# Token sums of the seven-product feed-forward layers issued earlier, from the rows, and a new order of the seven products

## The chip, the cores and the metric

The kernel runs on one core of one Trainium2 chip. The metric is device time in microseconds (us), from a run without a profile; the median of three runs is compared. TensorE (PE) does the matmuls, VectorE (DVE) and ScalarE (ACT) and GpSimd (POOL) work elementwise, and SyncE (SP) issues the loads.

## What is computed

Two blocks of two layers each on 512 tokens of width 1024. Each of the four layers has a mixer and a feed-forward part; the change touches three of the four feed-forward parts. The reference, cut to them:

```python
def rmsnorm(x, g):
    xf = x.astype(jnp.float32)
    y = xf * lax.rsqrt(jnp.mean(xf * xf, axis=-1, keepdims=True) + EPS)
    return (y * g).astype(x.dtype)

def swiglu_ffn(u, w_gate, w_up, w_down):        # w_gate, w_up: 1024 x 2816, w_down: 2816 x 1024
    return (jax.nn.silu(u @ w_gate) * (u @ w_up)) @ w_down

# first block, layer l:   x = x + g2 * _swiglu(_rms_norm(x, norm_ffn[l]) * (1 + sc2) + sh2, ...)
# second block, layer i:  h = h + swiglu_ffn(rmsnorm(h, ffn_norm[i]), ...)
```

## The kernel before

Activations are kept transposed: channels on the 128 partitions, 512 tokens along the row. The residual stands in `xT`, eight tiles `X[0]` to `X[7]` of 128 channels. Every operand of a matmul is split into two reduced-precision parts, `hi` (a cast on ACT) and `lo` (the difference, on DVE), and a product is three matmuls (`mm3`, L304 to L306): hi by hi, lo of the moving operand by hi, hi by lo of the weights. Weights are loaded by SP into three `raw` buffers and split by `split` (L296 ACT, L297 DVE).

A feed-forward part (`ffn(n, ...)`, n = 0 to 3) has 22 columns j of 128 hidden units. For each it makes a gate tile and an up tile (psum `pg`, `pu`), evacuates them to silu(gate) times up (`s`), and splits that into `d`. After every 5 or 6 columns (`PARTS_S`) come the eight down products (`dn`, psum `pj`) over these columns. Six PSUM banks serve `pg`, `pu` and `pj` in turn.

There are two ways to make a column. The **dense** way (`gu`) takes 48 matmuls of 512 tokens: 2 outputs, 8 channel tiles, 3 passes. The **seven-product** way (`gu7`, `seven`) works on quarters: gate and up weights by their first and second four channel tiles (g1, g2, u1, u2), and the tokens by their first and second 256. Seven products of quarter size, combined by additions, replace eight: 84 matmuls of 256 tokens. For this the weights need four sums (s1 to s4, DVE, per column) and the tokens need four sums `q[0]` to `q[3]` per pair of channel tiles (k, k+4), once per layer for four pairs: `crossed` (L679 to L698). They become `xh` and `xl` (hi and lo parts, 128x1024 each); `cross(i)` names the quarter sum i of all four pairs. `FIRST_S` says how many columns of a layer are dense: all 22 for n = 0, three for n = 1, one for n = 2 and for n = 3.

For n = 1 the norm is a `Split`: the normed rows are built in two halves of 256 tokens (`build`, L471 to L493: `z` on DVE, bias and hi on ACT, lo on DVE for even channel tiles and on POOL for odd ones), and the first two dense columns run half by half (`nm.lin`). For n = 2 and 3 the norm is a `Norm`: the rows are only scaled by the gain, and the reciprocal norm R multiplies the outputs. `finish` (L408) makes R: column sums on PE (`ss`), a chain of 13 small DVE instructions (`rsqrt`), four transposes on PE (`rb`) and a copy on ACT (`R`). It is called in the evacuation of the first column, so that nothing of that column leaves PSUM before R stands.

In `crossed` POOL adds hi and lo back to the row value `z` (L687, eight of 128x512, with three `z` buffers), DVE makes the four sums (L690 to L693, 128x256 each), ACT casts `xh` (L695) and DVE subtracts to `xl` (L696). It is called in the first `gu7`, so after the dense columns and their evacuation in program order. In `seven` the first product is g1 with a quarter of the plain rows; the second is with `cross(0)`, the third and fifth with `cross(1)` and `cross(2)`, the seventh with `cross(3)`, the fourth and sixth with plain rows. Products 1, 3, 5 and 7 share the quarter bank `r1`; after 1, 3 and 5 ACT copies it away (L733, L737, L740) before it is written again.

The program is written in the order of these items. A scheduler then orders each engine's queue from its own estimates; the queues run in order, and each instruction waits for its semaphores.

Of the kernel before, what the change touches and what calls it, by code (L numbers as in the profile page):

```python
# [10 lines left out]
F32 = mybir.dt.float32  # L11
# [3 lines left out]
OP = mybir.AluOpType  # L15
# [5 lines left out]
FIRST_S = (22, 3, 1, 1)  # L21
# [69 lines left out]
def _layout(i):  # L91
# [130 lines left out]
def _program(nc, tc, a, out, stages=STAGES):  # L222
# [207 lines left out]
    class Split:  # L430
        def __init__(self, eps, acol, shcol=None, ahead=None):
            self.eps, self.acol, self.shcol, self.ahead, self.W = eps, acol, shcol, ahead, None
            self.rstd = None
            self.h = []

# [36 lines left out]
        def build(self, hf):  # L472
            o = HALVES[hf]
            for c in range(KC):
# [3 lines left out]
                z = tmp("z")  # L478
# [200 lines left out]
    def crossed(h):  # L679


        out = []
        hv = T // 2
        for k in range(4):
            z1, z2 = tmp("z"), tmp("z")
            for z, c in ((z1, k), (z2, k + 4)):
                G.tensor_tensor(z, h[c][0].bitcast(F32), h[c][1].bitcast(F32), op=OP.add)  # L687
            t = wide1("ws")
            q = [t[:, i * hv:(i + 1) * hv] for i in range(4)]
            V.tensor_tensor(q[0], z1[:, :hv], z1[:, hv:], op=OP.subtract)  # L690
            V.scalar_tensor_tensor(q[1], z2[:, hv:], -1.0, q[0], op0=OP.mult, op1=OP.subtract)
            V.tensor_tensor(q[2], z2[:, hv:], z1[:, hv:], op=OP.subtract)
            V.scalar_tensor_tensor(q[3], q[1], -1.0, z2[:, :hv], op0=OP.mult, op1=OP.subtract)  # L693
            hi, lo = wide1("xh", F32R), wide1("xl", F32R)
            S.copy(hi, t)  # L695
            V.tensor_tensor(lo, t, hi.bitcast(F32), op=OP.subtract)  # L696
            out.append([(hi[:, i * hv:(i + 1) * hv], lo[:, i * hv:(i + 1) * hv]) for i in range(4)])
        return out  # L698
# [5 lines left out]
    def seven(g, u, h, x4):  # L704
# [5 lines left out]
        g1, s1, s2, s4, s3, g2, u1, u2 = [w[:, o:o + 512] for w in (wa, wb, wc, wd) for o in (0, 512)]  # L710
        for t, src in ((g1, g[:, :4]), (wd, u), (g2, g[:, 4:])):
            last_load[0] = nc.sync.dma_start(t, flat(src))
        V.tensor_tensor(s1, u1, u2, op=OP.add)
        ah, al = split(wa, 1024)
        V.tensor_tensor(s2, s1, g1, op=OP.add)
        V.tensor_tensor(s4, s2, g2, op=OP.add)  # L716
        bh, bl = split(wb, 1024)
# [16 lines left out]
        product(r3, ah, al, 4, cross(0), True)  # L734
        S.copy(bu[:, :hv], r3)
        product(r1, bh, bl, 0, cross(1), False)
        S.copy(ua[:, hv:], r1)  # L737
        product(r3, bh, bl, 4, quarter(4, two_), False)
        product(r1, ch, cl, 0, cross(2), False)
        S.copy(bu[:, hv:], r1)  # L740
        product(r2, ch, cl, 4, quarter(4, one_), False)
# [6 lines left out]
    def ffn(n, nm, gcol, nxt):  # L748
        sparse = FIRST_S[n] < FC
        phase("ffn" if sparse else "ffn0")  # L750
        x4 = []
        direct = isinstance(nm, Split)
        h = nm.h
        d = {}

        def gu(js):
            def it():
# [5 lines left out]
                if js[0] == 0 and direct:  # L763
                    nm.lin([gr[:2], gr[2:]])
                else:
                    lin(gr, h)
                if nm.R is None:
                    nm.finish().to_sbuf()
# [17 lines left out]
        def gu7(j):  # L786
            def it():
                if not x4:
                    x4.extend(crossed(h))
# [977 lines left out]
    if stages[0] != "mix0":  # L1767
        phase("ffn")
        consts()
        nc.sync.dma_start(row, a["row"].to_broadcast([128, NROW]))  # L1770
        if stages[0] in STAGES[:4]:
            cond()
            mods()
            _run(chain(md0.stream(range(24)), md1.stream(range(24))))
        nm = norms[stages[0]]().all()
# [43 lines left out]
```

## Time and profile before

| what | us |
|---|---|
| median of three runs | 2718.51 (2717.61 to 2718.73) |
| the profiled execution's own time | 2719.51 |
| its span, first to last instruction | 2717.7 |
| PE busy in the span | 2525.8 (93%) |
| DVE busy | 1987.6 (73%) |
| ACT busy | 1250.1 (46%) |
| POOL busy | 534.6 (20%) |

The three layers with seven products run at 945 to 1317 (n = 1), 1733 to 2102 (n = 2) and 2335 to 2703 (n = 3) us of the span. A window's row gives, for a stretch, the busy time of each engine with the number of instructions, and then PEclk: the granted TensorE clock as a share of 2.4 GHz, so 0.50 is the lower of its two levels (1.2 GHz) throughout. Idle time of an engine stands in square brackets before an instruction, with what ended it.

### The profile page before, as it was taken

The page shows a single profiled execution, that of the slowest core. Times are in us where ns is not written, and L with a number is a line of the kernel's source. Part 1 is how long each engine was busy: PE and PEld are TensorE (multiplying, and loading weights), DVE is VectorE, ACT ScalarE, POOL GpSimd, SP SyncE. Part 2 cuts the span into 40 slices and gives each one's busy share as a digit, 9 for nine tenths or more (in the row PEclk, how much of TensorE's full clock was granted, in tenths as well). Part 3 has the DMA queues.
Part 4 walks back from the last instruction along what each step waited for, and adds up shares of the span by engine and source line. Part 5 has one row for each costly group of instructions (what it writes and reads, how often), then busy time and mean ns, then how long its engine had stood idle before and what let it go on. Part 6 is the DMA issues. An engine that isn't in the chain of part 4 may idle for free.

```text
span 2717.7 us, 39747 instructions
## 1 busy us (share of the span) xinstructions
PE 2525.8 (93%) x15176; PEld 2229.9 (82%) x15176; DVE 1987.6 (73%) x3494; ACT 1250.1 (46%) x2283; POOL 534.6 (20%) x371
## 2 busy tenths in 40 slices
PE   5788989999999879999999999799999987799998
PEld 3666888888888879999788888599998877599997
DVE  7898765555457566667678786788777897778776
ACT  4456643222357534445455444345444544445443
POOL 3345120000113220000100000311013783301102
PEclk9988999999999989999999999899999998899999
DMA  7611025555420113323322121133233210133332
GB/s 263 229 54 39 32 95 200 177 174 190 133 88 24 47 55 106 104 93 103 95 78 72 61 72 61 50 103 107 97 102 109 69 56 16 60 111 99 100 98 85
DMA packets 93519, 265.78 MB, mean 98 GB/s; under 512 B 10256, under 2 KB 12688, under 8 KB 93328
## 3 DMA queue, kind: packets, MB, share of 16 engines
q1 hardware_dynamic: 93328, 263.24, 29.2%
q8 instruction: 119, 1.95, 0.3%
q14 instruction: 72, 0.59, 0.1%
HBM read 261.10 MB, written 2.10 MB: 97 GB/s over the span
## 4 chain that ended last, share of the span: by engine, by line
PE 75%; DVE 13%; issue 3%; POOL 3%; DMA 3%; ACT 3%; POOLq 0%; SPq 0%; DVEq 0%; ACTq 0%
PE pj L304 10%; PE pj L306 10%; PE pj L305 10%; PE pg L304 6%; PE pg L306 6%; PE pg L305 6%; PE pu L306 5%; PE pu L304 5%; PE pu L305 5%; POOL yp L1586 2%; DVE lo L297 2%; DMA araw<-ada 1%; PE pj L1398 1%; PE pj L1399 1%; PE pj L1400 1%
## 5 line engine op out<-in xcount | busy, mean ns | idle before, releaser
L296 ACT CAST hi<-raw 128x1024 fp32r<-128x1024 f32 (+5 forms) x445 | 392.9, 891 | 721.2 <-PE pj L305 262.4
L297 DVE TENSOR_TENSOR lo<-raw,hi 128x1024 fp32r<-128x1024 f32 (+5 forms) x435 | 462.2, 1068 | 146.8 <-ACT hi L296 144.3
L304 PE MATMUL pj<-d,hi 128*128 128x512 f32 (+1 forms) x940 | 353.2, 382 | 3.8 <-DVE xT L677 2.0
L305 PE MATMUL pj<-d,hi 128*128 128x512 f32 (+1 forms) x940 | 355.3, 378 | 0.0
L306 PE MATMUL pj<-d,lo 128*128 128x512 f32 (+1 forms) x940 | 352.8, 380 | 0.0
L745 POOL TENSOR_TENSOR bu<-bu 128x256 f32<-128x256 f32 x61 | 102.0, 1672 | 807.5 <-ACT bu L740 594.3
L304 PE MATMUL pu<-hi 128*128 128x256 f32 (+1 forms) x736 | 229.9, 312 | 3.3 <-DVE z L479 3.2
L306 PE MATMUL pu<-hi,lo 128*128 128x256 f32 (+1 forms) x736 | 229.5, 312 | 0.0
L305 PE MATMUL pu<-lo,hi 128*128 128x256 f32 (+1 forms) x736 | 229.4, 312 | 0.0
L305 PE MATMUL pj<-lo,hi 128*128 128x512 f32 (+2 forms) x520 | 208.0, 400 | 4.4 <-DVE lo L490 2.4
L304 PE MATMUL pj<-hi 128*128 128x512 f32 (+2 forms) x520 | 207.9, 403 | 3.9 <-ACT qk L887 1.2
L304 PE MATMUL pg<-xh,hi 128*128 128x256 f32 x732 | 206.8, 283 | 2.2 <-ACT hi L296 2.2
L304 PEld LDWEIGHTS pj<-d,hi 128*128 128x128 f32 x940 | 176.7, 189 | 38.5 <-DVE xT L677 2.6
L306 PE MATMUL pg<-xh,lo 128*128 128x256 f32 x732 | 206.5, 282 | 0.1
L305 PE MATMUL pg<-xl,hi 128*128 128x256 f32 x732 | 205.8, 281 | 0.0
L306 PE MATMUL pj<-hi,lo 128*128 128x512 f32 (+2 forms) x520 | 205.5, 396 | 0.3 <-DVE lo L297 0.3
L305 PEld LDWEIGHTS pj<-d,hi 128*128 128x128 f32 x940 | 177.3, 189 | 33.8 <-issue 1.0
L306 PEld LDWEIGHTS pj<-d,lo 128*128 128x128 f32 x940 | 177.3, 189 | 33.1 <-issue 0.5
L304 PE MATMUL pg<-hi 128*128 128x256 f32 (+1 forms) x564 | 188.3, 334 | 5.5 <-DVE z L479 4.4
L306 PE MATMUL pg<-hi,lo 128*128 128x256 f32 (+1 forms) x564 | 187.3, 332 | 2.2 <-DVE lo L297 2.2
L305 PE MATMUL pg<-lo,hi 128*128 128x256 f32 (+1 forms) x564 | 187.0, 332 | 0.6 <-DVE lo L490 0.6
L296 ACT CAST hi<-ws 128x1024 fp32r<-128x1024 f32 x122 | 126.9, 1048 | 112.7 <-DVE ws L716 34.8
(471 smaller groups left out, 6406.8 us busy)
## 6 DMA issues: line engine op xcount, KB each, us to landing
raw<-w_gu SPq DMA_DIRECT2D x115, 512.0 KB, 3.6
araw<-ada SPq DMA_DIRECT2D x96, 512.0 KB, 5.9
raw<-w_dn SPq DMA_DIRECT2D x48, 384.0 KB, 3.1
raw<-w_gu SPq DMA_DIRECT2D x61, 256.0 KB, 3.0
ws<-w_gu SPq DMA_DIRECT2D x61, 256.0 KB, 2.9
raw<-w_dn SPq DMA_DIRECT2D x48, 320.0 KB, 2.9
raw<-w_p SPq DMA_DIRECT2D x24, 512.0 KB, 3.5
raw<-w_out SPq DMA_DIRECT2D x32, 256.0 KB, 2.8
```

The source lines that it names most:

```text
L296: S.copy(hi, raw)
L297: (eng or V).tensor_tensor(lo, raw, hi.bitcast(F32), op=OP.subtract)
L304: E.matmul(ps, lh, rh, start=start, stop=False, **k)
L305: E.matmul(ps, lh, rl, start=False, stop=False, **k)
L306: E.matmul(ps, ll, rh, start=False, stop=stop, **k)
L745: G.tensor_tensor(bu[:, :hv], bu[:, :hv], bu[:, hv:], op=OP.add)
L1398: E.matmul(o, xh[:, ts], wh[:, k], start=st_, stop=False, skip_group_check=True)
L1399: E.matmul(o, xh[:, ts], wl[:, k], start=False, stop=False, skip_group_check=True)
L1400: E.matmul(o, xl[:, ts], wh[:, k], start=False, stop=sp, skip_group_check=True)
L1586: G.tensor_tensor(yp[:, sft:], yp[:, sft:], pr[:, sft:], op=OP.add)
```

## The change

- `FIRST_S` is (22, 3, 2, 2): layers 2 and 3 get a second dense column, in place of one of seven products.
- `crossed` handles one pair k at a time and is called from `gu`, right behind the matmuls of a dense column and ahead of its evacuation: for n = 1 all four pairs behind the first two columns, for n = 2 and 3 two pairs behind each of the two dense columns.
- The row values no longer come from hi + lo. For n = 2 and 3 ACT makes them from `X[c]` and the gain (eight of 128x512). For n = 1 `build` leaves its `z` tiles standing in eight buffers (`keep`); the first 256 tokens are filled by POOL from hi + lo, and the bias, where `build` had not added it, is added by ACT.
- `q[0]` and `q[2]` move from DVE to POOL; `xl` moves to POOL for k = 1 and 3.
- In `seven`, g1 and g2 share one raw buffer, loaded by one DMA of 512 KB in place of two of 256 KB, and are split together. The two products of plain rows with g1 and g2 come first. The order behind them is: `cross(0)` and `cross(1)` with s1 and s2, the plain quarter and `cross(2)` with s4 and s3, `cross(3)` with u2.
- The pools: a phase of its own for n = 1 with eight `z` buffers, six in place of three for n = 2 and 3.

The diff, cut to its core:

```diff
-FIRST_S = (22, 3, 1, 1)
+FIRST_S = (22, 3, 2, 2)
...
-                z = tmp("z")
+                z = self.keep[c] if self.keep else tmp("z")
...
+    def crossed(k, z1, z2, pool_lo):
         hv = T // 2
+        t = wide1("ws")
+        q = [t[:, i * hv:(i + 1) * hv] for i in range(4)]
+        G.tensor_tensor(q[0], z1[:, :hv], z1[:, hv:], op=OP.subtract)
+        G.tensor_tensor(q[2], z2[:, hv:], z1[:, hv:], op=OP.subtract)
+        V.scalar_tensor_tensor(q[1], z2[:, hv:], -1.0, q[0], op0=OP.mult, op1=OP.subtract)
+        V.scalar_tensor_tensor(q[3], q[1], -1.0, z2[:, :hv], op0=OP.mult, op1=OP.subtract)
+        hi, lo = wide1("xh", F32R), wide1("xl", F32R)
+        S.copy(hi, t)
+        (G if pool_lo else V).tensor_tensor(lo, t, hi.bitcast(F32), op=OP.subtract)
...
         product(r1, ah, al, 0, quarter(0, one_), True)
         S.copy(ua[:, :hv], r1)
-        product(r3, ah, al, 4, cross(0), True)
+        product(r2, ah, al, 4, quarter(4, one_), True)
+        product(r3, bh, bl, 0, cross(0), False)
         S.copy(bu[:, :hv], r3)
-        product(r1, bh, bl, 0, cross(1), False)
+        product(r1, bh, bl, 4, cross(1), False)
         S.copy(ua[:, hv:], r1)
-        product(r3, bh, bl, 4, quarter(4, two_), False)
-        product(r1, ch, cl, 0, cross(2), False)
+        product(r3, ch, cl, 0, quarter(4, two_), False)
+        product(r1, ch, cl, 4, cross(2), False)
         S.copy(bu[:, hv:], r1)
-        product(r2, ch, cl, 4, quarter(4, one_), False)
         product(r1, uh, ul, 0, cross(3), False)
...
+        def sums(ks):
+            for k in ks:
+                z = []
+                for c in (k, k + 4):
+                    if direct:
+                        z.append(nm.keep[c])
+                        if c % 2 == 0 and nm.shcol:
+                            S.activation(z[-1][:, T // 2:], z[-1][:, T // 2:], AF.Identity, bias=nm.shcol(c))
+                    else:
+                        z.append(tmp("z"))
+                        S.activation(z[-1], X[c], AF.Copy, scale=nm.gcol(c))
+                x4.append(crossed(k, *z, k % 2))
...
+                if sparse and len(x4) < 4:
+                    sums(range(4) if direct else range(2 * js[0], 2 * js[0] + 2))
                 if nm.R is None:
                     nm.finish().to_sbuf()
```

What this moves in the queues, at three places.

DVE in layer 1, just behind the last `lo` of the second half of the rows (lo_8624 in both). Before: the split of the third dense column's weights, the first evacuations, and the token sums (L690, ws) only behind the evacuation of that third column (s_8989).

```order
L297 TENSOR_TENSOR lo_8930<-raw_8927,hi_8929 128x1024
L775 TENSOR_TENSOR s_8913<-s_8913,pu_8645 128x512
L297 TENSOR_TENSOR lo_8936<-raw_8933,hi_8935 128x1024
L389 TENSOR_TENSOR d_8917<-s_8913,d_8916 128x512
L713 TENSOR_TENSOR raw_9048<-raw_9049 128x512
L775 TENSOR_TENSOR s_8920<-s_8920,pu_8659 128x512
L297 TENSOR_TENSOR lo_9057<-raw_9048,hi_9056 128x1024
L389 TENSOR_TENSOR d_8924<-s_8920,d_8923 128x512
L775 TENSOR_TENSOR s_8989<-s_8989,pu_8940 128x512
L690 TENSOR_TENSOR ws_9000<-z_8996 128x256
```

Of the change (there the third column's weights are lo_8978 and lo_8984, and its evacuation comes much later):

```order
L689 SCALAR_TENSOR_TENSOR ws_8923<-z_8664,ws_8923 128x256
L690 SCALAR_TENSOR_TENSOR ws_8923<-ws_8923,z_8664 128x256
L689 SCALAR_TENSOR_TENSOR ws_8932<-z_8665,ws_8932 128x256
L690 SCALAR_TENSOR_TENSOR ws_8932<-ws_8932,z_8665 128x256
L689 SCALAR_TENSOR_TENSOR ws_8943<-z_8666,ws_8943 128x256
L690 SCALAR_TENSOR_TENSOR ws_8943<-ws_8943,z_8666 128x256
L693 TENSOR_TENSOR xl_8929<-ws_8923,xh_8928 128x1024
L693 TENSOR_TENSOR xl_8949<-ws_8943,xh_8948 128x1024
L298 TENSOR_TENSOR lo_8978<-raw_8975,hi_8977 128x1024
L791 TENSOR_TENSOR s_8961<-s_8961,pu_8645 128x512
L689 SCALAR_TENSOR_TENSOR ws_8952<-z_8667,ws_8952 128x256
L298 TENSOR_TENSOR lo_8984<-raw_8981,hi_8983 128x1024
```

The sums now stand ahead of the third column's weights and of every evacuation.

ACT at the start of layer 3 (layer 2 is alike), behind the last cast of the rows (hi_22092 before, hi_21990 of the change). Before: R, the first evacuation, then the four casts of the sums.

```order
L733 COPY ua_22292<-pg_22290 128x256
L426 COPY R_22199<-rb_22194 128x512
L779 ACTIVATE s_22201<-s_22201 128x512
L388 CAST d_22207<-s_22201 128x512
L695 CAST xh_22220<-ws_22215 128x1024
L695 CAST xh_22233<-ws_22228 128x1024
```

Of the change (hi_22239 is the split of the first seven-product column's g1 and g2; L761 makes the row values):

```order
L297 CAST hi_22239<-raw_22233 128x1024
L761 ACTIVATE z_22064<-xT_70,vec_71 128x512
L761 ACTIVATE z_22066<-xT_70,vec_71 128x512
L761 ACTIVATE z_22077<-xT_70,vec_71 128x512
L761 ACTIVATE z_22079<-xT_70,vec_71 128x512
L692 CAST xh_22073<-ws_22068 128x1024
L692 CAST xh_22086<-ws_22081 128x1024
L427 COPY R_22123<-rb_22118 128x512
L761 ACTIVATE z_22197<-xT_70,vec_71 128x512
L761 ACTIVATE z_22199<-xT_70,vec_71 128x512
L761 ACTIVATE z_22210<-xT_70,vec_71 128x512
L761 ACTIVATE z_22212<-xT_70,vec_71 128x512
```

Two pairs go ahead of R, the row values of the other two stand behind it.

PE in layer 3, in the first seven-product column (pg_22259, pu_22260), between its products with `cross(2)` and `cross(3)`, of the change. Here the last matmul of `cross(2)` (weights hi_22251, lo_22252) and the two behind it:

```order
L305 MATMUL pg_22259<-xh_22219,hi_22251 128x256
L306 MATMUL pg_22259<-xl_22220,hi_22251 128x256
L307 MATMUL pg_22259<-xh_22219,lo_22252 128x256
L307 MATMUL pg_22389<-hi_21763,lo_22370 128x256
L305 MATMUL pg_22389<-hi_21770,hi_22369 128x256
```

and 22 matmuls of the next column (pg_22389, pu_22390) later the first of `cross(3)` (weights hi_22255, lo_22256):

```order
L307 MATMUL pu_22390<-hi_21990,lo_22370 128x256
L305 MATMUL pu_22390<-xh_22073,hi_22375 128x256
L306 MATMUL pu_22390<-xl_22074,hi_22375 128x256
L305 MATMUL pg_22259<-xh_22073,hi_22255 128x256
L306 MATMUL pg_22259<-xl_22074,hi_22255 128x256
```

In the program these two products stand next to each other; in the queue a part of the next column stands between them.

## Rows read from the trace of the kernel before

**Rows 1.** The page: busy time, and the granted clock in 40 slices.

```profile
PE 2525.8 (93%) x15176; PEld 2229.9 (82%) x15176; DVE 1987.6 (73%) x3494; ACT 1250.1 (46%) x2283; POOL 534.6 (20%) x371
PEclk9988999999999989999999999899999998899999
```

**Rows 2.** Windows: whole first parts, then steady sevens, then a dense column.

```profile
core 0: us, PE busy (x) PEld busy (x) DVE busy (x) ACT busy (x) POOL busy (x), PEclk, DMA share, GB/s
959.30:1035.30 76.00, 62.02 (x423) 57.49 (x422) 54.49 (x75) 34.76 (x55) 17.35 (x14) 0.87 0.20 63
1733.40:1819.90 86.50, 68.42 (x476) 63.72 (x477) 71.53 (x107) 39.44 (x61) 20.41 (x13) 0.86 0.22 69
2334.60:2420.90 86.30, 68.70 (x479) 63.91 (x478) 71.75 (x108) 37.34 (x59) 13.38 (x12) 0.86 0.22 71
1069.70:1128.10 58.40, 58.40 (x493) 58.38 (x492) 46.51 (x63) 33.70 (x57) 5.47 (x5) 1.00 0.32 104
...
2334.60:2345.50 10.90, 10.90 (x49) 9.01 (x48) 5.52 (x7) 1.69 (x3) 1.70 (x2) 1.00 0.00 0
...
1869.00:1909.00 40.00, 40.00 (x339) 40.00 (x338) 39.66 (x57) 24.55 (x42) 10.96 (x4) 1.00 0.31 104
```

**Rows 3.** Windows: the stretches of the token sums in layers 1, 2 and 3.

```profile
985.60:1010.00 24.40, 10.42 (x41) 7.74 (x40) 23.06 (x30) 9.60 (x12) 8.87 (x6) 0.63 0.12 44
1754.80:1776.00 21.20, 9.49 (x30) 7.14 (x31) 20.68 (x26) 7.35 (x9) 7.09 (x5) 0.50 0.15 50
2355.40:2376.00 20.60, 8.85 (x27) 6.50 (x28) 20.41 (x25) 7.34 (x9) 7.15 (x6) 0.50 0.15 52
```

**Rows 4.** PE's waits from 2345.5 to 2376: total us, times, longest.

```profile
PE pu L305 <- DVE xl L696: 8.1, 3, 3.6
PE pu L304 <- ACT xh L695: 7.9, 4, 5.0
PE rb L373 <- DVE rstd L361: 0.9, 1, 0.9
PE pg L304 <- ACT hi L296: 0.7, 1, 0.7
```

**Rows 5.** DVE's timeline, layer 3: start, us, instruction, [idle before].

```profile
2347.39 0.16 DVE L344 TENSOR_SCALAR rm<-ss 128x4 f32<-128x4 f32 x1 [7.27 <-PE ss L367]
...
2349.57 0.16 DVE L361 SCALAR_TENSOR_TENSOR rstd<-rt,rstd 128x4 f32<-128x4 f32 x1
2351.09 0.69 DVE L778 TENSOR_TENSOR s<-pg,R 128x512 f32<-128x512 f32 x1 [1.36 <-ACT R L426]
2351.70 0.68 DVE L780 TENSOR_TENSOR su<-pu,R 128x512 f32<-128x512 f32 x1
...
2352.29 0.41 DVE L690 TENSOR_TENSOR ws<-z 128x256 f32<-128x256 f32 x1
...
2357.31 2.28 DVE L696 TENSOR_TENSOR xl<-ws,xh 128x1024 fp32r<-128x1024 f32 x1
```

**Rows 6.** POOL's timeline in the same stretch.

```profile
2336.95 1.30 POOL L687 TENSOR_TENSOR z<-hi,lo 128x512 f32<-128x512 f32 x1 [1.95 <-DVE lo L383]
2354.12 4.39 POOL L687 TENSOR_TENSOR z<-hi,lo 128x512 f32<-128x512 f32 x3 [15.87 <-DVE ws L692]
```

**Rows 7.** Groups by form, 2326 to 2376: count, busy us, mean ns, idle before.

```profile
L382 ACT ACTIVATE hi<-xT,vec 128x512 fp32r<-128x512 f32 x8 | 5.2, 710 | 0.0
L695 ACT CAST xh<-ws 128x1024 fp32r<-128x1024 f32 x4 | 4.2, 1046 | 12.3 <-DVE ws L693 12.3
L297 DVE TENSOR_TENSOR lo<-ws,hi 128x1024 fp32r<-128x1024 f32 x2 | 2.4, 1222 | 0.0
```

**Rows 8.** ACT's timeline, layer 3: two copies out of PSUM.

```profile
2348.93 0.37 ACT L733 COPY ua<-pg 128x256 f32<-128x256 f32 x1 [10.06 <-PE pg L306]
2350.47 0.59 ACT L426 COPY R<-rb 128x512 f32<-128x512 f32 x1 [1.16 <-PE rb L373]
```

**Rows 9.** POOL's timeline, layer 1, second half of the rows.

```profile
961.83 1.78 POOL L487 TENSOR_TENSOR lo<-z,hi 128x256 fp32r<-128x256 f32 x2 [9.15 <-ACT hi L486]
964.38 0.75 POOL L487 TENSOR_TENSOR lo<-z,hi 128x256 fp32r<-128x256 f32 x1 [0.77 <-ACT hi L486]
965.74 0.74 POOL L487 TENSOR_TENSOR lo<-z,hi 128x256 fp32r<-128x256 f32 x1 [0.61 <-ACT hi L486]
```

**Rows 10.** POOL's sums `bu` of the columns: min/median/max ns.

```profile
L745 POOL TENSOR_TENSOR bu<-bu x61: 732/1107/6873, 1015.5 to 2674.8; 128x256 f32<-128x256 f32 x61
```

**Rows 11.** DVE's timeline, layer 1: the evacuation ahead of the sums.

```profile
986.43 0.69 DVE L775 TENSOR_TENSOR s<-s,pu 128x512 f32<-128x512 f32 x1 [7.17 <-ACT s L774]
```

More of the change, by code (lines that the diff above doesn't have):

```diff
@@ L434, in __init__ @@
             self.h = []
+            self.keep = None
         def square(self, c, o=slice(0, T)):
@@ L677, in add_x @@
             V.tensor_tensor(x, ps, x, op=OP.add)
-    def crossed(h):
-        out = []
+    def crossed(k, z1, z2, pool_lo):
         hv = T // 2
[L684 to L698, printed above, removed]
+        t = wide1("ws")
[7 more added lines that the diff above has]
+        (G if pool_lo else V).tensor_tensor(lo, t, hi.bitcast(F32), op=OP.subtract)
+        return [(hi[:, i * hv:(i + 1) * hv], lo[:, i * hv:(i + 1) * hv]) for i in range(4)]
     def wide1(tag, dt=F32):
@@ L709, in seven @@
         wb, wc = wide1("ws"), wide1("ws")
-        g1, s1, s2, s4, s3, g2, u1, u2 = [w[:, o:o + 512] for w in (wa, wb, wc, wd) for o in (0, 512)]
-        for t, src in ((g1, g[:, :4]), (wd, u), (g2, g[:, 4:])):
+        g1, g2, s1, s2, s4, s3, u1, u2 = [w[:, o:o + 512] for w in (wa, wb, wc, wd) for o in (0, 512)]
+        for t, src in ((wa, g), (wd, u)):
             last_load[0] = nc.sync.dma_start(t, flat(src))
+        ah, al = split(wa, 1024)
         V.tensor_tensor(s1, u1, u2, op=OP.add)
-        ah, al = split(wa, 1024)
         V.tensor_tensor(s2, s1, g1, op=OP.add)
+        bh, bl = split(wb, 1024)
         V.tensor_tensor(s4, s2, g2, op=OP.add)
-        bh, bl = split(wb, 1024)
         V.tensor_tensor(s3, g1, u1, op=OP.add)
@@ L749, in ffn @@
         sparse = FIRST_S[n] < FC
-        phase("ffn" if sparse else "ffn0")
+        direct = isinstance(nm, Split)
+        phase(("ffn1" if direct else "ffn") if sparse else "ffn0")
         x4 = []
-        direct = isinstance(nm, Split)
         h = nm.h
+        def sums(ks):
[10 more added lines that the diff above has]
+                x4.append(crossed(k, *z, k % 2))
         d = {}
@@ L763, in it @@
                 if js[0] == 0 and direct:
+                    if sparse:
+                        nm.keep = [tmp("z") for c in range(KC)]
+                        for z, (hi, lo) in zip(nm.keep, h):
+                            o = HALVES[0]
+                            G.tensor_tensor(z[:, o], hi[:, o].bitcast(F32), lo[:, o].bitcast(F32), op=OP.add)
                     nm.lin([gr[:2], gr[2:]])
@@ L787, in it @@
             def it():
-                if not x4:
-                    x4.extend(crossed(h))
                 hv = T // 2
@@ L1767, in _program @@
     if stages[0] != "mix0":
-        phase("ffn")
+        phase("ffn0")
         consts()
```

3 rows, old and new, of the table PHASES are left out of this document.

## The prediction

> **What bounds the kernel now.** I read the page first. PE is busy 93% of the span, and the granted clock is below full in a few slices only [rows 1]; so the time is PE's work plus the places where PE waits or runs slowly. In the three layers with seven products I then took windows. A steady stretch shows the pace: 493 matmuls of 256 tokens in 58.4 us at clock 1.00, 0.1185 us each, so a seven-product column of 84 takes 9.95 us; a dense column of 48 matmuls takes 10.9 [rows 2]. The first part of each layer is off that pace. In layer 1, 420 of the 423 instructions of its window are the columns' (48 of 512 tokens, 372 of 256); at the pace they take 11.0 + 44.1 = 55.1 us, the window has 76.0: 20.9 lost. In layer 3 it is 456 (48 and 408), 11.0 + 48.3 = 59.3 against 86.3: 27.0 lost; layer 2 is the same, 86.5 [rows 2].
>
> The loss is the token sums. While they are made PE is busy 10.4 of 24.4 us in layer 1, the clock stands at 0.63 of full there and at 0.50 in layers 2 and 3, and DVE is busy nearly throughout [rows 3]. PE waits for exactly two things, the casts `xh` and the differences `xl`: 16.0 of the 17.6 us of its waits in layer 3, each pair k in turn [rows 4]. The sums are late because of the queue: in layer 1 DVE sits idle 7.2 us and then starts with the evacuation of the third dense column [rows 11], the sums behind it; in layer 3 DVE waits 7.3 us for the column sums `ss`, does the chain for R and two evacuation steps, and only then makes the first sum, at 2352.3 [rows 5]. POOL stands idle 15.9 us with two of its eight additions done [rows 6].
>
> So in layer 3 the 27.0 us are 17.6 of waits, 2.2 for `ss` and `rb` on PE (1.7 of the 1.9 us from the end of the dense column to `rm` [rows 2, 5], and by estimate 0.5), and the rest, 7.2, is work at the lower clock.
>
> **The change part by part.** The profiled execution took 2719.5 us, its span 2717.7, the median 2718.5; I sum against 2719.5 and take off 1.0 at the end.
>
> *The second dense column* in layers 2 and 3 costs 10.9 - 9.95 = 1.0 us each, on PE, in full. It also gives the sums 10.9 us more cover, and the plain products of g1 and g2 (24 matmuls, 2.85 us) give 1.4 more than the 12 that stood ahead of the first sum before.
>
> *Layer 1.* The row values need nothing new but POOL's eight first-half sums of 256 tokens: 8 x 0.75 = 6.0 us, and POOL is idle 9.15 us just there [rows 9]; hidden, with 3 us to spare. The bias on ACT (four of 256 tokens, by the nearest row under 0.71 each [rows 7]) lies in time that ACT has. Then POOL makes the eight differences (6.0 us) and two `xl` of 128x1024: by [rows 6], 1.30 us for 512, I estimate 2.6 each. DVE makes eight of 0.41 and two `xl` of 1.22 [rows 5, 7]. The second half of the rows is done at 966.5 [rows 9], and PE has first the rest of two half columns and then, from 975, the third dense column until 986 [rows 11], then 2.85 us of plain products: 989. From 966 to 989 DVE has 5.7 us of sums and 11.6 of other work (five `lo` of 1.22, eight instructions of 0.69). That fits, with 5 us for waits. What is late next is the third column's own weights: their `lo` now stands behind six sums and two `xl` on DVE, which start when POOL's fifth difference lands (about 969), and one `xl` on POOL (2.6 us) may fall between them: 969 + 6 x 0.34 + 2 x 1.14 + 1.2 = 974.5, and 977.1 with POOL, against 975.2 when PE wants it: up to 2 us of waiting, and about as much at the lower clock if it is the longer one. I take 3 lost of the 20.9: **18 us gained** (bounds 12, if the sums too come some 5 us late, and 20).
>
> *Layers 2 and 3*, by layer 3, counted from the start of the first dense column (2334.6). PE: column one to 10.9, `ss` to 12.6, column two with `rb` in it to 24.0, plain products to 26.9. There it wants the sums. Pairs 0 and 1: ACT's row values (0.65 pitch by [rows 7]) and POOL's differences are done by 11, while DVE idles; but DVE's own part stands behind `rm`, which waits for `ss` (12.8). The chain for R takes 2.3 us [rows 5], four sums in it 1.4, `xl` 1.2: 17.7, well covered. Pairs 2 and 3 are not covered. Their row values stand on ACT behind the copy of R; R needs `rb`, which stands on PE behind 35 of the 48 matmuls of column two: 12.6 + 7.9 = 20.6, so R is there at 21.9 (from the end of `rstd` to the end of that copy it was 1.3 us [rows 5, 8]). Four row values end at 24.5, POOL's last difference at 25.6. DVE then has four sums, one `s`, one `su`, two products and the weight sums s1 and s2, 4.4 us, to 30.0; the cast of these weights lands at 30.1. **PE waits 3.2 us.** Their `lo` comes behind `xl` of pair 2 and a `d`, at 32.9: 2.3 more. The `xl` of pair 3 is on POOL, and POOL gets in where DVE pauses for a cast, at 34.6: 37.1, and PE waits 2.3 again. In sum 7.8 us in place of 17.6. For the clock I take the same share, 7.2 x 7.8 / 17.6 = 3.2, and 1 us because DVE is the second limit here: busy 39.66 of 40 us while PE runs without a gap [rows 2], so it has nothing to catch up with. Loss after: 2.2 + 7.8 + 3.2 + 1.0 = 14.2, and the extra column 1.0: **11.8 us gained** in each of the two. Bounds: 23.8 with no wait at all, 5 with the rival POOL starved.
>
> *POOL and DVE in each other's way.* The same POOL sum of 256 tokens takes 0.73 us at best and 6.87 at worst [rows 10], an `xl` on DVE 2.28 where it is 1.22 alone, just while POOL runs three additions [rows 5 to 7]. So each holds the other up, and the change takes POOL's share of the sums from 8 instructions to 18 in layer 1 and to 10 in layers 2 and 3, two of them of 128x1024. The Trainium skill (SBUF — State Buffer, "SBUF: two separate sides") says that the two engines share one pair of ports by an exclusive lock held for a whole instruction, against a DVE instruction with two inputs in SBUF too. By that rule work moved to POOL is not free even where POOL idles; the trace agrees, with the 6.87 us above. Where it decided, the time would be that of the rival named POOL starved.
>
> *The new order of products and the loads.* One DMA less per column, the same bytes; nothing waits for loads in a steady stretch. DVE has the same instructions per column; the sums s1 to s4 are wanted later than before. I cost this at nothing; the cover is PE's gapless run at 9.95 us per column, and if it fails the price is that of the rival named slower.
>
> Sum: 18 + 2 x 11.8 = 41.6; 2719.5 - 41.6 = 2677.9, and as a median **2677 us**.
>
> **The rivals.**
>
> *Full cover.* My walk down the queues is too gloomy (the scheduler meant the sums to be ready), nothing waits and the clock stays at 2.4 GHz: 20 + 2 x 23.8 = 67.6, 2651 us. For it: DVE idles over 5 us in column one, and the casts are short. Against: pairs 2 and 3 stand behind R by the order.
>
> *POOL starved.* POOL's last `xl` meets DVE's back-to-back work and waits as the `bu` sums do, up to 6.9 us [rows 10], in place of the 2.9 that I gave it; 4 us more of waits and 2 at the lower clock in each of layers 2 and 3 (5.8 gained), 12 in layer 1: 23.6, 2695 us.
>
> *Slower: a copy exposed in every column.* The products with `cross(2)` and `cross(3)` both write `r1`, now back to back in the program, with ACT's copy between. If PE waited for it, it would pay from the last matmul to the end of the copy: 0.37 us for the copy [rows 8], with the hand-overs on both sides 0.8 to 1.0. In 59 seven-product columns that is 47 to 59 us, against 41.6 gained: up to 2735. It decides where fewer than 7 to 8 matmuls (0.9 us) stand between. The order shows 22 at the place printed and 12 or more in all, 1.4 us; so against it.
>
> *It does not do what it says.* The sums are issued early but their last step ends as late as before, since DVE is the limit: the waits stay, and only the 1.0 us is paid: within 0.2%, about 2716 to 2722. Against: the sums stand ahead of the evacuations in the queue, and PE has 12.3 us more of work before it wants them.
>
> **How the numbers follow.** The forecast (2664 to 2687) has 0.55, full cover (2651 to 2664) 0.16, POOL starved (2687 to 2705) 0.20, no change 0.04, slower 0.05. The range 2655 to 2702 leaves out a part of the second, a little of the third, and the last two, under 0.2 together. Faster by over 0.2% (5.4 us, about what a measurement can tell here) is 0.91, same 0.04, slower 0.05.
>
> **What would show it.** In the profile after, in layer 1's first part: PE's wait for `xh` and `xl` gone, a wait of up to 2.4 us before the third dense column, clock 1.00 through it. In layers 2 and 3: the two dense columns end 24 us after the start, then three waits of 2 to 3 us each, the first for the cast of the weights' sums, the last for POOL's `xl`; the clock at 1.2 GHz for some 7 us in place of the 21 and more of [rows 3]. Steady columns stay at 9.95 us. The prediction is wrong if the row values of pairs 2 and 3 come ahead of R in fact, if POOL's `xl` takes over 5 us, or if a steady column takes over 10.2.

## The result, and the profile after

The changed kernel took 2672.2 us (median of 4 runs, 2670.1 to 2680.7) beside 2718.6 of the kernel before, run with it: a ratio of 0.9834, 95% interval 0.9811 to 0.9857, a gain of 46.4 us. Run again later it took 2677.4 beside 2718.7: 0.9852 (0.9829 to 0.9874), 41.4 us. The forecast was 2677, 2655 to 2702.

The profiled execution is the slowest of the first four (2680.65 us, span 2678.9), and it was 3.8 us late where layer 1 begins, before any changed code. So I compare stretches, not ends. The page of the changed kernel, its busy time and granted clock, beside [rows 1]:

```profile
PE 2519.2 (94%) x15104; PEld 2222.2 (83%) x15104; DVE 1951.8 (73%) x3448; ACT 1255.4 (47%) x2291; POOL 557.1 (21%) x383
PEclk9889999999999999999999999999999997999999
```

The clock row cuts the span into 40 slices, each digit in tenths of 2.4 GHz. The three slices in which it fell to 8 around the token sums (the 15th, 26th and 35th) are 9 now. DVE is busy 36 us less than before, POOL 22 more.

For every kernel below I give the **first part** of each layer: from its first gate or up matmul to the first such matmul behind the first eight down products (five or six columns), and the sum of **parts two and three** of the three layers, which hold nothing but seven-product columns and down products. Each first part, and each of the later ones, has the same number of gate, up and down matmuls in all kernels with the same `FIRST_S`. All times are starts of matmuls in the trace, in us:

```
                     layer 1  layer 2  layer 3   parts 2 and 3, three layers
before                 124.0    120.8    120.3   510.3
changed kernel         110.7    105.1    105.2   512.1
the same, again        108.4    105.2    104.3   513.5
sums_only              109.2    112.8    113.6   510.5
order_only             121.0    119.1    119.4   512.0
first_only             123.4    119.7    119.6   510.3
old_order              107.1    108.4    109.2   510.3
rows_early             108.7    107.3    104.9   511.8
late_half              106.9    105.2    104.4   513.3
no_pool                105.8    110.0    108.4   512.8
weights_first          108.6    106.8    106.0   513.7
mixed                  105.8    105.3    106.9   510.9
mixed_old_order        105.6    112.6    110.5   510.3
copy_twice             108.6    104.4    104.3   512.3
```

The gain is all in the first parts: 13.4 + 15.7 + 15.1 = 44.2 us in the first profile (15.6 + 15.6 + 16.0 in the second), less 1.8 to 3.2 us in the columns behind. PE's longest waits in layer 1, then all in layer 3, from the first matmul to where the down products run alone (engine, tile, line, what it waited for: total, times, longest), where [rows 4] stood before:

```profile
PE pu L305 <- DVE z L481: 3.2, 1, 3.2
PE pg L305 <- ACT hi L297: 2.1, 1, 2.1
PE pg L307 <- DVE lo L298: 1.8, 1, 1.8
PE rb L471 <- DVE rstdh L362: 1.2, 1, 1.2
...
PE pu L305 <- ACT hi L297: 2.7, 1, 2.7
PE pu L307 <- DVE lo L298: 2.0, 1, 2.0
PE pu L306 <- POOL xl L693: 0.3, 1, 0.3
```

In layer 3 the seven waits for `xh` and `xl` (16.0 us) are gone but for 0.3, and 4.7 us for the first column's own weights (`hi`, `lo`) have come. In layer 1 the 3.2 us for `z` were there before; the other three are new. Windows of the first part, in layer 1 from behind `rb`, in layer 3 from its first matmul, both to where the down products run alone, then of the two stretches at the lower clock in layers 2 and 3 (columns as in [rows 2]), where [rows 3] stood:

```profile
964.60:1034.40 69.80, 65.96 (x465) 62.09 (x465) 52.79 (x67) 36.87 (x61) 21.68 (x17) 0.98 0.23 73
...
2308.60:2388.10 79.50, 74.58 (x485) 68.62 (x484) 61.61 (x95) 41.59 (x64) 26.56 (x14) 0.96 0.22 70
...
1753.20:1760.00 6.80, 4.63 (x21) 4.04 (x20) 5.69 (x7) 3.46 (x5) 5.24 (x1) 0.50 0.21 77
2340.30:2347.10 6.80, 5.70 (x25) 5.41 (x26) 5.69 (x7) 3.26 (x5) 4.83 (x1) 0.50 0.22 77
```

The mean granted clock of these windows is 0.98 and 0.96, and 1.2 GHz was granted for 6.8 us in layers 2 and 3 each, where the stretches of [rows 3] showed it for over 20.

### The profile page after: what moved, and what is told of

It reads as the page before. It is cut to its first block, busy times and chain, and to the rows that moved or that the text cites. A ratio compares the mean times of both kernels' runs of the same rounds, so it can differ in the third digit from the quotient of the medians.

```text
span 2678.9 us, 39465 instructions
## 1 busy us (share of the span) xinstructions
PE 2519.2 (94%) x15104; PEld 2222.2 (83%) x15104; DVE 1951.8 (73%) x3448; ACT 1255.4 (47%) x2291; POOL 557.1 (21%) x383
## 4 chain that ended last, share of the span: by engine, by line
PE 71%; DVE 15%; issue 4%; POOL 3%; DMA 3%; ACT 3%; DVEq 0%; SPq 0%; POOLq 0%; ACTq 0%
PE pj L305 10%; PE pj L306 10%; PE pj L307 10%; PE pg L305 5%; PE pg L307 5%; PE pg L306 5%; PE pu L307 4%; PE pu L305 4%; PE pu L306 4%; DVE lo L298 3%; DMA raw<-w_gu 2%; POOL yp L1600 1%; PE pj L1412 1%; PE pj L1413 1%; PE pj L1414 1%
## 5 line engine op out<-in xcount | busy, mean ns | idle before, releaser
L741 POOL TENSOR_TENSOR bu<-bu 128x256 f32<-128x256 f32 x59 | 110.7, 1876 | 774.1 <-ACT bu L737 760.5
L305 PE MATMUL pg<-xh,hi 128*128 128x256 f32 x708 | 199.1, 281 | 1.2 <-ACT ua L734 1.1
L307 PE MATMUL pg<-xh,lo 128*128 128x256 f32 x708 | 198.1, 280 | 0.0
L306 PE MATMUL pg<-xl,hi 128*128 128x256 f32 x708 | 198.0, 280 | 0.0
```

What stands on the lines that cost most here:

```text
L305: E.matmul(ps, lh, rh, start=start, stop=False, **k)
L306: E.matmul(ps, lh, rl, start=False, stop=False, **k)
L307: E.matmul(ps, ll, rh, start=False, stop=stop, **k)
L741: G.tensor_tensor(bu[:, :hv], bu[:, :hv], bu[:, hv:], op=OP.add)
```

## The experiments

### What each part of the change is worth

**sums_only**: the changed `crossed`, `sums` and pools, with the old `seven` and one dense column.

```diff
-FIRST_S = (22, 3, 2, 2)
+FIRST_S = (22, 3, 1, 1)
...
-                    sums(range(4) if direct else range(2 * js[0], 2 * js[0] + 2))
+                    sums(range(4))
```

> The early token sums alone: from the rows, ahead of the evacuations, two of four on GpSimd; one dense column in layers 2 and 3 as before, old order of products and old loads. Theory (the sums' place in the queue is the cause): layer 1 keeps nearly its whole gain, 12 us; in layers 2 and 3 PE wants the sums some 14 us after the start of the dense column and has the last of them at about 23, so about 9 of 17.6 us of waits stay, 7 us gained each; together 26, about 2692 us (2684 to 2700). Rival (the second dense column and the order of products make the gain, by the cover that they give): under 8 us gained in all, above 2710.

Measured: 2688.4 us beside 2718.4, 0.9888 (0.9875 to 0.9902): 30.0 us gained, as the queue theory had it (26), layer 1 better than expected (14.8) and layers 2 and 3 at 8.0 and 6.7. PE's waits in layer 3, all but 0.5 us:

```profile
PE pu L306 <- POOL xl L693: 5.4, 2, 3.1
PE rb L374 <- DVE rstd L362: 1.6, 1, 1.6
PE pu L306 <- DVE xl L693: 1.4, 1, 1.4
PE pg L305 <- ACT hi L297: 1.4, 1, 1.4
PE pu L305 <- ACT xh L692: 0.7, 1, 0.7
```

Without the second dense column PE still waits there for the sums, POOL's two `xl` above all. This run moves three things together: the sums' place in the queue, where the row values come from, and POOL's share. **no_pool**, below, takes the last away; the first two no run separates.

**order_only**: the kernel before with the changed `seven` alone (the part of the diff ahead with `product`, and g1 and g2 in one load). **first_only**: the kernel before with one line changed:

```diff
-FIRST_S = (22, 3, 1, 1)
+FIRST_S = (22, 3, 2, 2)
```

> The kernel before with the new order of the seven products and g1 and g2 in one load, nothing else. Theory (it only gives 1.4 us more cover ahead of the sums in each of three layers): 2712 to 2719 us, about 2715. Rival (the copy of the quarter bank between the products with cross(2) and cross(3) is waited for in every seven-product column): 47 to 59 us slower, above 2760. Second rival (the new order is itself a large part of the gain, since s1 to s4 are wanted later): under 2708.

> The kernel before with a second dense column in layers 2 and 3, nothing else. DVE's queue keeps all token sums behind the evacuations of both dense columns. Theory (the queue decides, not the cover): nothing gained, 1.0 us paid for each of the two columns, 2720 to 2722 us. Rival (10.9 us more work on PE covers as much of the sums wherever they stand): 10 to 20 us faster, 2698 to 2710.

Measured: order_only 2716.1, 0.9989 (0.9979 to 0.9998), 2.3 us gained: cover only, and not slower. Its first parts are 0.9 to 3.0 us shorter, its later parts 1.7 longer. In layer 3 the many waits for `xh` and `xl` have become one, for the cast of the first column's s1 and s2, which DVE makes behind most of the token sums:

```profile
PE pu L304 <- ACT hi L296: 18.7, 1, 18.7
PE pu L306 <- DVE lo L297: 1.0, 1, 1.0
```

first_only 2712.0, 0.9978 (0.9969 to 0.9987), 6.4 us gained where I had expected 2 lost and the rival 10 to 20 gained. Neither was right. Its first parts are 0.6, 1.1 and 0.7 us shorter; the waits for the sums are all still there (layer 3):

```profile
PE pu L304 <- ACT xh L695: 9.4, 4, 5.8
PE pu L305 <- DVE xl L696: 5.7, 3, 2.6
```

That is 15.1 us, where 16.0 stood in [rows 4]; the wait of 0.9 for `rb` is gone, since R's chain now runs beside the second dense column. So 10.9 us more work ahead of the sums covered some 2 us, twice what the column costs; the queue decides, not the cover. The other 4 us of the median I can't place: this execution was already 5.3 us earlier than that of before where layer 1 begins, with the same program up to there.

**old_order**: the changed kernel with the `seven` of before, the same part of the diff undone:

```diff
-        product(r2, ah, al, 4, quarter(4, one_), True)
-        product(r3, bh, bl, 0, cross(0), False)
+        product(r3, ah, al, 4, cross(0), True)
...
+        product(r2, ch, cl, 4, quarter(4, one_), False)
         product(r1, uh, ul, 0, cross(3), False)
```

> The changed kernel with the old order of the seven products and the old loads. Theory (1.4 us less cover in each of three layers, some of it multiplied by the lower clock): 2 to 6 us slower than the changed kernel's 2672, so 2674 to 2678. Rival (the new order exposes copies or loads somewhere in the steady columns): faster than the changed kernel, under 2670.

Measured: 2678.5, 0.9853 (0.9840 to 0.9867), beside the changed kernel's 2672.2 and 2677.4. By the first parts the new order gives 3.2 to 4.9 us in each of layers 2 and 3, takes 1.3 to 3.6 in layer 1, and takes 1.8 to 3.2 in the later parts: a net of 1 to 4, made of larger terms of both signs. As a time it can't be told from nothing: the intervals overlap. In sum: the early sums 30 us, the second dense column with them 10 (from sums_only to old_order), the order of products and loads 1 to 6.

### What holds the rest

**after_again** is the changed kernel, **rows_early** makes all eight row values of layers 2 and 3 behind the first dense column:

```diff
+        def rows(ks):
+            for k in ks:
+                for c in (k, k + 4):
+                    zs[c] = tmp("z")
+                    S.activation(zs[c], X[c], AF.Copy, scale=nm.gcol(c))
...
+            if not direct and not zs:
+                rows(range(4))
```

> The changed kernel as it is, to have it beside the next three and to narrow its interval: 2668 to 2676 us, about 2672.

> The changed kernel with all eight row values of layers 2 and 3 made by ACT ahead of the copy of R (eight z buffers, one su), nothing else. Theory of the prediction (pairs 2 and 3 are late because their row values stand behind R, and DVE's work piles up behind them): the wait for the cast of s1 and s2 (2.66) falls to about 0.5, that for their lo (1.9) stays near 2 since the evacuations are still ahead of it on DVE, and the lower clock gives back some 1.5: 3 to 4 us a layer, about 2665 us. Rival (the row values are on time anyway and the waits come from the evacuations ahead of s1 and s2 on DVE alone): within 2 us of the changed kernel.

Measured: after_again 2677.4 (0.9852), a little above the 2668 to 2676 expected; rows_early 2677.4 (0.9856, 0.9831 to 0.9881). The 3 to 4 us a layer didn't come, as the rival had it: the row values of pairs 2 and 3 were done 8 us sooner, and the waits in layer 3, below, are the same within 0.5 us each. In layer 2 they come to 6.4 us for 4.8, and its first part is 2.1 us longer.

```profile
PE pu L305 <- ACT hi L297: 2.5, 1, 2.5
PE pu L307 <- DVE lo L298: 1.7, 1, 1.7
PE pu L306 <- POOL xl L693: 0.8, 1, 0.8
```

That the row values' place costs nothing is not shown by this. The edit, which also takes one of the two `su` buffers away, made DVE's second `xl` meet POOL's and take 3.14 us for 1.22, so DVE came to the evacuations 23.9 us after the start of layer 3 in place of 21.9. DVE in rows_early, then in the changed kernel, where it waited for R:

```profile
2326.89 3.14 DVE L693 TENSOR_TENSOR xl<-ws,xh 128x1024 fp32r<-128x1024 f32 x1 [0.19 <-ACT xh L692]
```

```profile
2330.55 0.69 DVE L794 TENSOR_TENSOR s<-pg,R 128x512 f32<-128x512 f32 x1 [3.10 <-ACT R L427]
```

**weights_first** goes one step on: also s1 and s2 of the first seven-product column ahead of the evacuations of both dense columns.

```diff
+                if sparse and js[-1] == FIRST_S[n] - 1:
+                    pre[js[-1] + 1] = weights7(*(a[f"w_gu{n}"][js[-1] + 1][:, i] for i in range(2)))
...
+                if late:
+                    with tc.issue_after(wmark[0].ins):
+                        evac([0], late[:], R)
+                        evac(js, gr, R)
```

> The changed kernel with the row values early (as in rows_early) and, in layers 2 and 3, the weight sums s1 and s2 of the first seven-product column made ahead of the evacuations of both dense columns; nothing else. Theory formed from rows_early (the two evacuations that stand ahead of s1 and s2 on DVE are the wait): the waits for the cast (2.6) and for its lo (2.0) fall under 0.7 together, one stretch of the lower clock goes, 5 to 6 us gained in each of the two layers, 10 to 12 us faster than the changed kernel, about 2664. Rival (POOL's xl of the last pair, up to 5.2 us long, is what comes next): it takes their place, within 3 us of the changed kernel.

Measured: 2681.1, 0.9859 (0.9840 to 0.9879), no better than the changed kernel. The wait for `hi` fell from 2.7 to 0.9 us, and others took its place; not POOL's `xl`, as the rival had it. In layer 2, below, they are for copies that stand behind other work on ACT, the longest behind a cast that itself waited 2.7 us for DVE; in layer 3 they are for `lo` of weights (1.8 and 1.0). PE's longest waits in layer 2:

```profile
PE pu L305 <- ACT bu L739: 2.3, 1, 2.3
PE pg L305 <- ACT ua L736: 1.7, 1, 1.7
PE pu L305 <- ACT hi L297: 0.9, 1, 0.9
```

DVE's timeline there shows what the order met (start, us, instruction), and POOL's beside it:

```profile
1739.69 1.22 DVE L693 TENSOR_TENSOR xl<-ws,xh 128x1024 fp32r<-128x1024 f32 x1
1741.10 3.15 DVE L693 TENSOR_TENSOR xl<-ws,xh 128x1024 fp32r<-128x1024 f32 x1 [0.19 <-ACT xh L692]
...
1755.40 2.88 DVE L712 TENSOR_TENSOR ws<-raw 128x512 f32<-128x512 f32 x1
```

```profile
1740.20 2.97 POOL L693 TENSOR_TENSOR xl<-ws,xh 128x1024 fp32r<-128x1024 f32 x1 [3.30 <-ACT xh L692]
...
1754.39 3.34 POOL L693 TENSOR_TENSOR xl<-ws,xh 128x1024 fp32r<-128x1024 f32 x1 [8.40 <-ACT xh L692]
```

The earlier work meets POOL's `xl` and takes 3.15 us for 1.22, and a sum of 128x512 takes 2.88 for 0.68. These rows suggest that what is left after the change is the amount of DVE's and POOL's work on the same stretch, not its order; no run shows it alone.

### POOL's share

**no_pool** makes on DVE what the change had moved to POOL in `crossed`.

```diff
-        G.tensor_tensor(q[0], z1[:, :hv], z1[:, hv:], op=OP.subtract)
-        G.tensor_tensor(q[2], z2[:, hv:], z1[:, hv:], op=OP.subtract)
+        V.tensor_tensor(q[0], z1[:, :hv], z1[:, hv:], op=OP.subtract)
+        V.tensor_tensor(q[2], z2[:, hv:], z1[:, hv:], op=OP.subtract)
...
-        (G if pool_lo else V).tensor_tensor(lo, t, hi.bitcast(F32), op=OP.subtract)
+        V.tensor_tensor(lo, t, hi.bitcast(F32), op=OP.subtract)
```

> The changed kernel with the two sums of each pair and both differences that it had moved to POOL made on DVE. Theory (DVE is the limit behind R, so 2.9 us more work on it there, less some 2 us that POOL's share now costs DVE by holding it up): 0 to 3 us slower in each layer, 2673 to 2680, about 2676. Rival POOL starved (POOL's share costs DVE more than it saves): faster than the changed kernel, under 2668.

Measured: 2682.1, 0.9869 (0.9845 to 0.9893), 4.7 us slower than after_again, run with it, though the intervals overlap. Neither theory nor rival was right, since the sum hides two signs: layers 2 and 3 are 4.8 and 4.1 us longer (the wait for `hi` grows to 6.1), layer 1 is 2.6 us shorter. For layer 1, DVE's groups by form from 960 to 1000 us say why. The changed kernel, then no_pool (count, busy us, mean ns):

```profile
L693 DVE TENSOR_TENSOR xl<-ws,xh 128x1024 fp32r<-128x1024 f32 x2 | 4.5, 2259 | 0.0
L689 DVE SCALAR_TENSOR_TENSOR ws<-z,ws 128x256 f32<-128x256 f32 x4 | 3.3, 821 | 0.6 <-POOL ws L687 0.6
L690 DVE SCALAR_TENSOR_TENSOR ws<-ws,z 128x256 f32<-128x256 f32 x4 | 3.0, 738 | 0.1
```

```profile
L693 DVE TENSOR_TENSOR xl<-ws,xh 128x1024 fp32r<-128x1024 f32 x4 | 4.8, 1219 | 0.4 <-ACT xh L692 0.4
L688 DVE TENSOR_TENSOR ws<-z 128x256 f32<-128x256 f32 x4 | 2.2, 552 | 0.0
L687 DVE TENSOR_TENSOR ws<-z 128x256 f32<-128x256 f32 x4 | 1.6, 414 | 0.0
L689 DVE SCALAR_TENSOR_TENSOR ws<-z,ws 128x256 f32<-128x256 f32 x4 | 1.6, 413 | 0.0
L690 DVE SCALAR_TENSOR_TENSOR ws<-ws,z 128x256 f32<-128x256 f32 x4 | 1.5, 413 | 0.0
```

With POOL's help DVE is busy 4.5 + 3.3 + 3.0 = 10.8 us with ten instructions; alone it makes all twenty in 11.7. POOL worked some 14 us to save DVE 0.9.

Layers 2 and 3 say little of POOL's share, since the edit moved something else there. In PE's queue `rb` stands behind 50 matmuls after `ss` in no_pool, in place of 35, so R comes 25.1 us after the start of layer 3 for 21.9. ACT's copy of R, in the changed kernel, then in no_pool:

```profile
2329.93 0.59 ACT L427 COPY R<-rb 128x512 f32<-128x512 f32 x1 [2.48 <-PE rb L374]
```

```profile
2334.57 0.59 ACT L427 COPY R<-rb 128x512 f32<-128x512 f32 x1 [6.63 <-PE rb L374]
```

R is 3.2 us later, and the wait for `hi` is 3.4 longer. From R to the end of s2 DVE needs 6.9 us alone and 6.7 with POOL's help. So the run shows that R stands on the path there, and gives no sign that POOL's share is worth anything in these layers.

**late_half** takes POOL's eight first-half sums of layer 1 (L777) away from the norm's chain.

```diff
-                        for z, (hi, lo) in zip(nm.keep, h):
-                            o = HALVES[0]
-                            G.tensor_tensor(z[:, o], hi[:, o].bitcast(F32), lo[:, o].bitcast(F32), op=OP.add)
                     nm.lin([gr[:2], gr[2:]])
+                    if sparse:
+                        o = HALVES[0]
+                        with tc.issue_after(nm.gmark.ins):
+                            for z, (hi, lo) in zip(nm.keep, h):
+                                G.tensor_tensor(z[:, o], hi[:, o].bitcast(F32), lo[:, o].bitcast(F32), op=OP.add)
```

> The changed kernel with POOL's eight first-half sums of layer 1 issued behind its last difference of the second half, nothing else. Theory (while POOL adds, DVE's small norm chain is held up: its 128x2 steps took 0.65 to 0.77 us in place of 0.16, and PE waited 1.23 for rb; and the third column's lo stood behind the sums): both waits of 1.2 and 1.8 us go, 2 to 4 us faster than the changed kernel, about 2669. Rival (layer 1 is held by the loads of the column behind, the 2.6 us that DVE waited for raw): the two waits go and a later one grows by as much, within 1 us.

Measured: 2676.1, 0.9847 (0.9823 to 0.9871), beside after_again's 2677.4: not to be told apart as a time. In the trace the mechanism is plain. The chain in the changed kernel, and in late_half, on DVE:

```profile
959.55 0.16 DVE L345 TENSOR_SCALAR rm<-ss 128x2 f32<-128x2 f32 x1 [1.11 <-PE ss L462]
959.75 0.70 DVE L350 TENSOR_SCALAR ri<-rm 128x2 int32<-128x2 int32 x1
...
961.18 1.35 DVE L358 SCALAR_TENSOR_TENSOR rt<-rj,rh 128x1 f32<-128x1 f32 x2
962.56 0.66 DVE L362 SCALAR_TENSOR_TENSOR rstdh<-rt,rj 128x2 f32<-128x2 f32 x1
963.26 0.35 DVE L358 SCALAR_TENSOR_TENSOR rt<-rstdh,rh 128x1 f32<-128x1 f32 x2
```

```profile
959.44 0.17 DVE L350 TENSOR_SCALAR ri<-rm 128x2 int32<-128x2 int32 x1
...
959.85 0.35 DVE L358 SCALAR_TENSOR_TENSOR rt<-rj,rh 128x1 f32<-128x1 f32 x2
960.23 0.16 DVE L362 SCALAR_TENSOR_TENSOR rstdh<-rt,rj 128x2 f32<-128x2 f32 x1
```

and POOL in the changed kernel, in the same stretch:

```profile
956.45 6.75 POOL L777 TENSOR_TENSOR z<-hi,lo 128x256 f32<-128x256 f32 x8
```

While POOL adds (to 963.2) the same steps take 0.66 to 0.70 for 0.16 and 1.35 for 0.35; from 963.26 on they are short again. The wait for `rb` (1.2) and that for the third column's `lo` (1.8) are gone in late_half, as expected; 1.1, 1.0 and 0.4 us for the first seven-product column have come, where POOL's part of the sums is 6 us later. Layer 1 is 1.5 us shorter than in after_again, under the 2 to 4 expected: most of what went came back further on, as the rival had it, though not for loads.

**mixed** is weights_first with `no_pool`'s edit in layer 1 alone; **mixed_old_order** is that with the `seven` of before.

```diff
-                x4.append(crossed(k, *z, k % 2))
+                x4.append(crossed(k, *z, not direct and k % 2, not direct))
```

> As weights_first, and in layer 1 the four sums and both differences of POOL back on DVE. Theory (in layer 1 POOL's share costs more than it saves, as the first part of no_pool showed: 105.8 against 108.4 to 110.7 us): 3 to 4 us faster than weights_first, about 2660. Rival (no_pool's layer 1 was a lucky execution): the same as weights_first.

> As mixed, with the old order of the seven products and the old loads. Theory (once the sums are early, the 1.4 us of cover of the new order is not needed, and its copies, waited for some 2 us in all, and its loads cost a little): 0 to 4 us faster than mixed, about 2658. Rival (the cover is still needed): 4 to 8 us slower than mixed.

Measured: mixed 2676.9, 0.9840 (0.9825 to 0.9855), 4.2 us faster than weights_first, run with it, where 3 to 4 was expected; as times the intervals overlap, but layer 1 is 105.8 again (105.6 in mixed_old_order): no lucky execution. It doesn't come to the 2660 expected and as a time doesn't beat the changed kernel; it carries the edit of weights_first in layers 2 and 3, and its layer 3 is 1.7 to 2.6 us longer. mixed_old_order 2688.1, 0.9887 (0.9871 to 0.9904): the rival held, and by more than it said. Without the cover of 12 more plain matmuls layers 2 and 3 are 7.3 and 3.6 us longer, though s1 and s2 are early: PE waited 3.3 for `hi` and, in layer 2, 5.3 for POOL's `xl`. The changed kernel with layer 1's sums on DVE, and nothing else, was not run; by these first parts I estimate that it would be some 3 us faster.

### The copy behind cross(2)

**copy_twice** makes the copy of the quarter bank between the products with `cross(2)` and `cross(3)` twice.

```diff
+        S.copy(bu[:, hv:], r1)
         product(r1, uh, ul, 0, cross(3), False)
```

> The changed kernel with ACT's copy of the quarter bank after the product with cross(2) made twice, 0.37 us more between it and the product with cross(3) in each of 59 columns. Theory (12 or more matmuls, 1.4 us, stand between in the queue, so the copy is hidden): 0 to 4 us slower than the changed kernel. Rival (the copy is exposed in every column): 59 x 0.37 = 22 us slower, about 2695.

Measured: 2676.0, 0.9836 (0.9820 to 0.9851), the same as the changed kernel. The 59 x 0.37 = 22 us more of copying are hidden in whole; the rival falls. Of the other copies of this bank the run says nothing.

## Why the prediction was right, step by step

- **What bounds** was read rightly: sums that come late by their place in the queue. Made early, they gave 30 of the 41 to 46 us (sums_only); the cover alone (first_only, order_only) gave 2 to 6.
- **Layer 1, forecast 18.** 13.4 in the first profile, 15.3 to 15.6 in the four other executions with the same layer 1. The wait for the third column's `lo`, forecast at up to 2, is 1.8. The step that failed is "hidden, with 3 us to spare": I had read POOL's idle time ahead of the second half of the rows, but not what DVE does in it, the norm's chain, and PE waited 1.2 us for its end (late_half shows both). With it fell "DVE makes eight of 0.41 and two `xl` of 1.22": beside POOL they took 0.82, 0.74 and 2.26. With these sums on DVE alone layer 1 gains 18.2, the forecast number, by another way than forecast. The 2.1 us for `hi` of the second seven-product column come from a load, which I had costed at nothing: DVE's weight sums waited for it until 997.92. It took 5.2 us from issue to landing, and 4.7, 3.3 and 3.2 in after_again, rows_early and copy_twice, where PE's wait is 1.6, none and none. The layer is no shorter for that (108.4, 108.7, 108.6): the two without the wait ran 10.2 us of it at the lower clock, after_again 3.4. The sign "clock 1.00 through it" failed in the first profile, where 1.2 GHz was granted for 3.4 us behind that wait.

```profile
997.92 0.69 DVE L710 TENSOR_TENSOR ws<-raw 128x512 f32<-128x512 f32 x1 [2.57 <-DMA raw<-w_gu]
```

- **Layers 2 and 3, forecast 11.8 each.** 15.7 and 15.1. The walk down the queues was right in order: three waits, the first for the cast of s1 and s2 (2.7, forecast 3.2), the second for their `lo` (1.9 and 2.0, forecast 2.3), the third for POOL's `xl`. The third is the term sized worst: 0.3 for 2.3. POOL's `xl` took 5.24 us, over the 5 that I had named as the sign of being wrong, but it began at 2339.89, 31.3 after the start where I had put 34.6, and ended at 36.5 (forecast 37.1), when PE, at 1.2 GHz by then, had only just come to it. I had added up waits and slow work; here the slow work filled the wait.

```profile
2339.89 5.24 POOL L693 TENSOR_TENSOR xl<-ws,xh 128x1024 fp32r<-128x1024 f32 x1 [5.65 <-ACT xh L692]
```

  The second term too large is `ss` and `rb`: 0.9 of the 2.2 went, as first_only shows. The lower clock was forecast for some 7 us and came for 6.8. The cause that I gave for these waits has two parts. That R, and so `rb` behind 35 matmuls on PE, stands on the path is borne out: R came at 21.9 as forecast, and with R 3.2 us later in no_pool the wait for `hi` grew by 3.4. That the row values behind R are what counts is not borne out: rows_early made them early and nothing was gained, though it also made DVE and POOL meet. In the changed kernel DVE pauses only 0.45 us between R and the `lo` of s1 and s2, and evacuations, sums and weight sums fill these 10 us; weights_first shows that putting s1 and s2 ahead of the evacuations doesn't help. Which part of that work decides stays open.
- **Order and loads at nothing.** Wrong by a few us: parts two and three of the layers take 510.3 to 510.5 us with the old order in all five kernels that have it, 510.9 to 513.7 in the nine executions with the new one; whether the order or the loads do it no run separates. PE's waits for ACT's copies show a part of it, not always: none in these parts of the first profile (there 0.5 us for a `lo` of weights), 1.5 us in layer 2 of after_again, whose 3.2 us more all lie in that layer. The longest are of the bank after `cross(1)`; the one below is the first profile's, in a fourth part. So the "slower" rival is not what this is: the copy that it named, after `cross(2)`, is hidden (copy_twice), and the price is some 2 to 3 us for its 47 to 59, under 0.1 us for each column of these parts.

```profile
2623.45 0.39 PE L305 MATMUL pg<-xh,hi 128*128 128x256 f32 x1 [1.06 <-ACT ua L734]
```

- **The rivals.** Full cover: no, 4.8 and 4.9 us of waits are left in layers 2 and 3. POOL starved: its mechanism is real, and in layer 1 POOL's share costs some 3 us; in layers 2 and 3 POOL's `xl` does come late by it (5.24 us), but PE waits 0.3 for it. The Trainium skill (SBUF — State Buffer, "SBUF: two separate sides"), weighed in the prediction, says that a DVE instruction with two inputs in SBUF and a GpSimd one that reads SBUF exclude each other for a whole instruction. The trace agrees: a DVE step of 0.16 us with two inputs (`rstdh`) took 0.66, near one POOL addition of 0.73. But `ri`, a step with one input, took 0.70 for 0.17 as well, which the rule on two inputs does not cover.
- The **sum** of 41.6 lies near the 42 to 44 us of the two profiles' stretches because a shortfall of 2 to 5 us in layer 1 and of 2 to 3 in the steady columns stood against 7 to 8 more in layers 2 and 3. That it lies so near is luck in part; that the gain is in these stretches, and why, was forecast.

## What to carry to other kernels

Where a short step is late because of its place in an in-order queue, moving it ahead paid once here, up to the point where the engine's own work filled the stretch; after that another order only changed the name of the wait. Work moved to GpSimd to unburden VectorE saved VectorE 0.9 us where it ran back to back, and cost the layer some 3: look at what VectorE does in GpSimd's idle time before you call it free. An edit to one engine's work can move another engine's instruction in its queue, as it moved `rb` on PE in no_pool: read the queues before you put a difference down to the edit. Before a gain of a few us is put down to an edit, compare stretches of the trace, since executions of one program differ by that much in code that nobody touched.

## What the runs showed that I had not expected

- A chain of tiny VectorE instructions pays dearly for GpSimd's company: `rm` to `rstdh` took 2.3 us before and 4.8 beside eight additions, one of which takes 0.73.
- The stretch ahead of layer 1, the same program in every kernel here, ended between 940.4 and 949.7 us in the profiled executions; what differs are stretches of 3.4 to 17 us at the lower clock, which come at other places each time, and waits of PE in the first 70 us (4.9 us for a cast in the profile of before, 1.7 in that of first_only).
